# Low halves of the weight tiles made by adding transfers from DRAM instead of by VectorE, in a hybrid encoder layer on one core

## The chip, the core and the metric

The kernel runs on one core of a Trainium2 chip. The metric is the device time of one execution in microseconds. The core's engines that matter here are TensorE (PE: matrix products), VectorE (DVE), ScalarE (ACT), GpSimd (POOL) and SyncE (SP), which issues most transfers; ScalarE and GpSimd can issue transfers too.

## The reference

One layer of a streaming encoder, in single precision, for 1024 prompt tokens and 32 tokens of a running stream (1056 in all), width 1024:

```python
h = _rmsnorm(x, norm_mix_g)
proj = jnp.einsum('bld,de->ble', h, w_in)          # 1024 -> 5136 columns
# A: y_a = a_b * causal_conv3(a_c * a_v)
# B: conv4 and silu on xbc, a Mamba-2 scan in chunks, gated RMSNorm with z
# C: gated unit, causal 31-tap convolution, LayerNorm, silu
x = x + jnp.einsum('ble,ed->bld', jnp.concatenate([y_a, y_b, y_c], axis=-1), w_out)
h2 = _rmsnorm(x, norm_ffn_g)
up, gate = jnp.split(jnp.einsum('bld,df->blf', h2, w_up), 2, axis=-1)
g_conv, new_f = _causal_dwconv(gate, st_f, conv_ffn_w)
x = x + jnp.einsum('blf,fd->bld', jax.nn.silu(g_conv) * up, w_down)   # 2816 -> 1024
```

A final RMSNorm follows, and the last inputs of each convolution and the scan's state are outputs too.

## The kernel before

Features lie on the 128 partitions, tokens along the free axis in three chunks of 256, 384 and 416. The matrix work is cut into *units*: 128 columns of a weight matrix by 1024 rows (a block of 512 KB; for `w_down` 128 rows by 1024 columns). There are 122 such units and one small one for the step widths, numbered in the order of the program: 0 to 19 the inputs of groups A and C, 20 the step widths, 21 to 32 the scan's x, B and C, 33 to 40 z, 41 to 48 the first half of the output projection (`o1`), 49 to 56 its second half (`o2`), then the FFN: two pairs of gate and up, the two `w_down` units of the pair before, two gates and ups again, and so on, with four down units at the end (119 to 122).

Every product of single precision is made of three products of a rounded format: with weights w = hi + lo and tokens x = xH + xL, `three` (L243 to L250) adds hi·xH (L245), hi·xL (L249) and lo·xH (L250) for each of the eight 128x128 blocks k of a unit. A unit is so 72 products. For a down unit the same three stand at L1236, L1237 and L1238, and its eight blocks are the eight output features m, taken in turn for all three chunks; two down units go together, block by block.

The halves are made by `convert` (L180 to L206) from a raw block that `load` (L165 to L178) has brought by a transfer on SyncE's queue: ScalarE rounds the raw block to `hi` (L205), then VectorE makes `lo` as raw minus `hi` (L200). Unit 0 alone is done by VectorE entirely. `weights` (L208 to L216) converts the next unit at the start of this unit's product; in front of a pair of down units two are converted at the start of the pair's second up product. `first_products` (L580 on) takes the first four units chunk by chunk while the next tokens are still prepared, so units 1 to 3 are converted close to each other. The units of `o1` take their blocks in the order 4 to 7, then 0 to 3 (L1130).

Raw blocks, `hi`, `lo` and token rows all live in a common pool of `SLOTS` = 44 tiles of about 4 KB per partition; a new tile waits until the users of the slot's earlier tile are done.

Around it: background work (convolutions, the scan) is put in small steps between the chunks of products, by a table of shares (`PUMP`). The scan fetches a tile `E` by a transfer and masks it on GpSimd (L819), and makes `xe` on GpSimd (L856); GpSimd also copies the state of a convolution into the buffers' heads (L475, L477: `gb` in the FFN) and the last inputs out (L482, L483). A scheduler sets each engine's order from the program's order; each engine then works through its own list in order, waiting for semaphores.

## Time and profile before

| | |
|---|---|
| time, median of 2 runs | 1555.62 us (1555.62 to 1555.63) |
| the profiled execution, first to last instruction | 1557.1 us, 23101 instructions |
| mean granted TensorE clock | 0.994 |
| TensorE busy | 1532.8 us (98%) |
| VectorE busy | 970.5 us (62%) |
| ScalarE busy | 467.5 us (30%) |
| GpSimd busy | 88.3 us (6%) |
| SyncE's and other hardware queues | 117.95 MB, 25.8% of 16 DMA engines |

Busy times count the instructions of an engine; issuing a transfer is not counted. A timeline row reads: start in us, duration in us, engine, line, operation, out<-in, shape, count, and in brackets how long the engine sat idle before it and what it waited for. "ACT hi L205" as a releaser is ScalarE's instruction that wrote `hi` on line 205. Rows with "SPq" or "ACTq" are issues of transfers: the time is that of the issuing, not of the transfer.

### The profile page before, as it was taken

How to read it: one execution, taken by the hardware profiler on the slowest of the kernel's cores; microseconds unless marked ns; L12 is line 12 of the kernel's file. 1: busy time of each engine (PE TensorE's matmuls, PEld its weight loads, DVE VectorE, ACT ScalarE, POOL GpSimd, SP SyncE). 2: the span in 40 equal slices, each digit the busy share in tenths (PEclk: the TensorE clock that was granted, in tenths of full speed). 3: DMA queues.
4: the chain of work that ended last, by engine and by line, in shares of the span. 5: the costliest groups of instructions: out<-in, count | busy, mean ns of one | idle time of the engine just before them, and what ended most of it. 6: DMA issues, size and time to landing. Idle time of an engine off the chain costs nothing.

```text
span 1557.1 us, 23101 instructions
## 1 busy us (share of the span) xinstructions
PE 1532.8 (98%) x9677; PEld 1502.3 (96%) x9677; DVE 970.5 (62%) x1397; ACT 467.5 (30%) x754; POOL 88.3 (6%) x213
## 2 busy tenths in 40 slices
PE   7999999999999899999999999999999999999998
PEld 7999999999999889999999999999999999999997
DVE  7467979599577479686654644545453544546455
ACT  6412112443656365153321120302111121202122
POOL 0000100011122021000000000000000000000000
PEclk9999999999999999999999999999999999999999
DMA  5603011311344577551211111111111111111102
GB/s 175 205 28 109 16 55 45 79 41 41 87 114 100 138 221 187 163 188 55 70 40 41 55 41 41 55 41 55 41 41 41 55 41 55 41 41 55 41 15 112
DMA packets 156758, 119.42 MB, mean 77 GB/s; under 512 B 9045, under 2 KB 145135, under 8 KB 156655
## 3 DMA queue, kind: packets, MB, share of 16 engines
q1 hardware_dynamic: 156639, 117.95, 25.8%
q8 instruction: 76, 1.25, 0.3%
q14 instruction: 27, 0.22, 0.0%
q10 hardware_dynamic: 16, 0.00, 0.0%
HBM read 97.08 MB, written 20.86 MB: 76 GB/s over the span
## 4 chain that ended last, share of the span: by engine, by line
PE 62%; DMA 1%; DVE 0%; ACT 0%; issue 0%; POOL 0%; SPq 0%; DVEq 0%; ACTq 0%; POOLq 0%
PE g L250 12%; PE g L245 12%; PE g L249 12%; PE g L1238 4%; PE g L1236 4%; PE g L1237 4%; PE xT L250 3%; PE xT L249 3%; PE xT L245 3%; PE xT L1236 1%; PE xT L1238 1%; PE xT L1237 1%; DMA zr<-zd 0%; DMA E<-acd 0%; PE yd L893 0%; PE st L883 0%
## 5 line engine op out<-in xcount | busy, mean ns | idle before, releaser
L245 PE MATMUL g<-hH,hi 128*128 128x416 f32 (+2 forms) x952 | 309.7, 325 | 0.0
L250 PE MATMUL g<-hH,lo 128*128 128x416 f32 (+2 forms) x952 | 307.3, 323 | 0.0
L249 PE MATMUL g<-hL,hi 128*128 128x416 f32 (+2 forms) x952 | 307.3, 323 | 0.0
L249 PE MATMUL g<-fL,hi 128*128 128x384 f32 (+2 forms) x792 | 255.9, 323 | 0.0
L250 PE MATMUL g<-fH,lo 128*128 128x384 f32 (+2 forms) x792 | 255.6, 323 | 0.0
L245 PE MATMUL g<-fH,hi 128*128 128x384 f32 (+2 forms) x792 | 255.6, 323 | 0.0
L245 PEld LDWEIGHTS g<-hH,hi 128*128 128x128 f32 x952 | 179.8, 189 | 1.8 <-issue 1.2
L249 PEld LDWEIGHTS g<-hL,hi 128*128 128x128 f32 x952 | 179.8, 189 | 0.4
L250 PEld LDWEIGHTS g<-hH,lo 128*128 128x128 f32 x952 | 179.6, 189 | 0.5 <-DVE lo L200 0.2
L290 DVE SCALAR_TENSOR_TENSOR cacc<-cb,par,cacc 128x1086 f32<-128x1086 f32 (+1 forms) x120 | 159.2, 1327 | 7.3 <-ACT cacc L287 5.7
L200 DVE TENSOR_TENSOR lo<-raw,hi 128x1024 fp32r<-128x1024 f32 x122 | 149.2, 1223 | 21.0 <-ACT hi L205 20.9
L249 PEld LDWEIGHTS g<-fL,hi 128*128 128x128 f32 x792 | 149.4, 189 | 0.4 <-issue 0.2
L250 PEld LDWEIGHTS g<-fH,lo 128*128 128x128 f32 x792 | 149.4, 189 | 0.5 <-issue 0.2
L245 PEld LDWEIGHTS g<-fH,hi 128*128 128x128 f32 x792 | 149.4, 189 | 0.3
L285 ACT ACTIVATE ca<-gb,par 128x1058 f32<-128x1058 f32 x22 | 26.0, 1182 | 407.8 <-DVE gb L1198 407.8
L1240 DVE TENSOR_TENSOR res<-res,g 128x416 f32<-128x416 f32 (+2 forms) x186 | 96.2, 522 | 60.7 <-PE g L1238 54.4
L1236 PE MATMUL g<-mH,hi 128*128 128x384 f32 (+2 forms) x396 | 129.0, 326 | 0.0
L1238 PE MATMUL g<-mH,lo 128*128 128x384 f32 (+2 forms) x396 | 128.5, 324 | 0.0
L1237 PE MATMUL g<-mL,hi 128*128 128x384 f32 (+2 forms) x396 | 128.0, 323 | 0.0
L205 ACT ACTIVATE hi<-raw 128x1024 fp32r<-128x1024 f32 x121 | 124.3, 1046 | 11.4 <-DMA raw<-in_w_in_dram 6.7
L1198 DVE TENSOR_TENSOR gb<-g,rf 128x384 f32<-128x384 f32 (+2 forms) x77 | 29.7, 410 | 142.4 <-PE g L250 142.4
L250 PE MATMUL xT<-fH,lo 128*128 128x256 f32 (+2 forms) x264 | 85.1, 323 | 0.0
(331 smaller groups left out, 2627.5 us busy)
## 6 DMA issues: line engine op xcount, KB each, us to landing
raw<-in_w_up_dram SPq DMA_DIRECT2D x44, 512.0 KB
raw<-in_w_in_dram SPq DMA_DIRECT2D x40, 512.0 KB
raw<-in_w_down_dram SPq DMA_DIRECT2D x22, 512.0 KB
E<-acd SPq DMA_DIRECT2D x16, 512.0 KB
xTd<-xn SPq DMA_DIRECT2D x8, 528.0 KB
zr<-zd SPq DMA_DIRECT2D x8, 528.0 KB
xm<-xTd SPq DMA_DIRECT2D x8, 528.0 KB
res<-r1d SPq DMA_DIRECT2D x8, 528.0 KB
```

The lines of the kernel that those rows point to most:

```text
L200: v.tensor_tensor(out=lo, in0=r, in1=hi.bitcast(F32), op=ALU.subtract)
L205: act.activation(hi, r, AF.Copy)
L245: pe.matmul(o, hi[:, k, :], x, start=first, stop=False)
L249: pe.matmul(o, hi[:, k, :], y, start=False, stop=False)
L250: pe.matmul(o, lo[:, k, :], x, start=False, stop=last)
L285: act.activation(out[:, u:u + n], buf[:, b:b + n], AF.Copy, scale=w_of(0))
L290: v.scalar_tensor_tensor(out=out[:, u:u + n], in0=buf[:, b + j:b + j + n], scalar=w_of(j), in1=out[:, u:u + n], op0=ALU.mult, op1=ALU.add)
L1198: v.tensor_tensor(out=buf[:, b:b + n], in0=ps[:, o:o + n], in1=rf[:, c0 + o:c0 + o + n], op=ALU.mult)
L1236: pe.matmul(o, hi[:, m, :], a[:, c0:c0 + w], start=(f == some[0]), stop=False)
L1237: pe.matmul(o, hi[:, m, :], b[:, c0:c0 + w], start=False, stop=False)
L1238: pe.matmul(o, lo[:, m, :], a[:, c0:c0 + w], start=False, stop=(f == some[-1]))
L1240: v.tensor_tensor(out=rc, in0=rc, in1=o, op=ALU.add)
```

## The change

The function `convert` no longer calls VectorE for `lo` (but for unit 0). ScalarE writes minus `hi` into `lo`, and four transfers on GpSimd's queue each read two of the unit's eight blocks (128 KB) from the weights in DRAM again and add them onto that: lo = -hi + w. So `lo` becomes ready in four pieces, and the product of a block waits for its own piece. The raw block has one reader less. The pool has 43 slots instead of 44, and `dynamic_dma_scratch_size` is 2048 instead of 1024. The lines after the function stand five lines further down than before. (The diff also removes all comments; those lines are left out here.)

```diff
-SLOTS = 44
+SLOTS = 43
...
             act.activation(hi, r, AF.Copy)
-            low()
+            act.activation(lo, hi.bitcast(F32), AF.Copy, scale=-1.0)
+            q3 = lo.rearrange("p (k m) -> p k m", m=P)
+            srcs = units[n][2]
+            for j in range(0, 8, 2):
+                s = srcs[j // 4][:, j % 4:j % 4 + 2, :] if len(srcs) == 2 else srcs[0][:, j:j + 2, :]
+                pool.dma_start(out=q3[:, j:j + 2, :], in_=s, accum_op=ALU.add)
...
-    nc = _bacc.Bacc("TRN2", target_bir_lowering=False, num_devices=1, dynamic_dma_scratch_size=1024)
+    nc = _bacc.Bacc("TRN2", target_bir_lowering=False, num_devices=1, dynamic_dma_scratch_size=2048)
```

The order of the instructions in three places. First ScalarE where two down units (65 and 66) are converted, at the start of the up product of unit 64; `ca` and `pf` are tiles of the FFN's gate and product, the L1203 row is the SiLU. Before:

```order
L205 ACTIVATE hi64_7897<-raw64_7714 128x1024 [waits DMAHW6_49,PE_49]
L285 ACTIVATE ca_7895<-gb_7892,par_77 128x1058 [waits DVE_49,Activation_49,Pool_49]
L205 ACTIVATE hi65_7992<-raw65_7807 128x1024 [waits DMAHW7_49,PE_49]
L205 ACTIVATE hi66_7996<-raw66_7901 128x1024 [waits DMAHW0_49,Activation_49]
L1203 ACTIVATE ca_7895<-ca_7895 128x1058 [waits DVE_49]
L1218 ACTIVATE mH3_8081<-pf_7896 128x1056 [waits DVE_49,Activation_49]
```

And of the change:

```order
L205 ACTIVATE hi64_8145<-raw64_7958 128x1024 [waits DMAHW6_49]
L206 ACTIVATE lo64_8146<-hi64_8145 128x1024 [waits Activation_49]
L290 ACTIVATE ca_8143<-gb_8140,par_77 128x1058 [waits DVE_49,PE_49,Pool_49]
L205 ACTIVATE hi65_8244<-raw65_8055 128x1024 [waits DMAHW7_49]
L206 ACTIVATE lo65_8245<-hi65_8244 128x1024 [waits Activation_49]
L205 ACTIVATE hi66_8252<-raw66_8153 128x1024 [waits DMAHW0_49,PE_49]
L1208 ACTIVATE ca_8143<-ca_8143 128x1058 [waits DVE_49]
L206 ACTIVATE lo66_8253<-hi66_8252 128x1024 [waits DMASW1_49,DMASW2_49,DMASW0_49,DMASW3_49,PE_49,Activation_49]
```

Each rounding is now followed by a negation, and the SiLU of the gate stands between the rounding and the negation of the second down unit. Next GpSimd at the same place. Before, it only fills and empties the heads of the convolution's buffers:

```order
L482 COPY fpack_7330<-gb_7705 128x2 [waits DVE_49]
L483 COPY fpack_7330<-gb_7705 128x2 [waits DVE_49]
L475 MEMSET gb_7892 128x2 [waits PE_49,Activation_49]
L477 COPY gb_7892<-par_77 128x2
L482 COPY fpack_7330<-gb_7892 128x2 [waits DVE_49]
L483 COPY fpack_7330<-gb_7892 128x2 [waits DVE_49]
```

And of the change:

```order
L487 COPY fpack_7554<-gb_8140 128x2 [waits DVE_49]
L488 COPY fpack_7554<-gb_8140 128x2 [waits DVE_49]
L211 DMA lo65_8245<-in_w_down_dram 128x256 [waits DMASW4_49,Activation_49,Pool_49]
L211 DMA lo65_8245<-in_w_down_dram 128x256 [waits DMASW5_49]
L211 DMA lo65_8245<-in_w_down_dram 128x256 [waits DMASW6_49]
L211 DMA lo65_8245<-in_w_down_dram 128x256 [waits DMASW7_49]
L211 DMA lo66_8253<-in_w_down_dram 128x256 [waits DMASW0_49,Activation_49]
L211 DMA lo66_8253<-in_w_down_dram 128x256 [waits DMASW1_49]
L211 DMA lo66_8253<-in_w_down_dram 128x256 [waits DMASW2_49]
L211 DMA lo66_8253<-in_w_down_dram 128x256 [waits DMASW3_49]
L480 MEMSET gb_8547 128x2 [waits DMAHW0_49]
L482 COPY gb_8547<-par_77 128x2
```

Eight transfers stand in a row there, the second unit's behind the first one's, and the next buffer's head behind all eight. Each transfer waits for the one that stood eight transfers earlier (DMASW0 to DMASW7 are their semaphores). Last GpSimd in the scan, where the first units of `o1` (41 and 42) are converted. Before, it has only the scan's own tiles there:

```order
L856 TENSOR_TENSOR xe_5075<-xd_5071,dend_2363 128x512 [waits DVE_49]
L856 TENSOR_TENSOR xe_5148<-xd_5144,dend_2363 128x512 [waits DVE_49]
L819 AFFINE_SELECT E_5112<-E_5112 128x1024 [waits DMAHW0_49]
L819 AFFINE_SELECT E_5264<-E_5264 128x1024 [waits DMAHW7_49,Activation_49]
L856 TENSOR_TENSOR xe_5313<-xd_5309,dend_2363 128x512 [waits DVE_49]
```

And of the change:

```order
L861 TENSOR_TENSOR xe_5235<-xd_5231,dend_2443 128x512 [waits DVE_49]
L861 TENSOR_TENSOR xe_5308<-xd_5304,dend_2443 128x512 [waits DVE_49]
L211 DMA lo41_5119<-in_w_out_dram 128x2x128 [waits DMASW4_49,Activation_49]
L211 DMA lo41_5119<-in_w_out_dram 128x2x128 [waits DMASW5_49]
L211 DMA lo41_5119<-in_w_out_dram 128x2x128 [waits DMASW6_49]
L211 DMA lo41_5119<-in_w_out_dram 128x2x128 [waits DMASW7_49]
L861 TENSOR_TENSOR xe_5477<-xd_5473,dend_2443 128x512 [waits DVE_49]
L824 AFFINE_SELECT E_5272<-E_5272 128x1024 [waits DMAHW0_49]
L211 DMA lo42_5326<-in_w_out_dram 128x2x128 [waits DMAHW6_49,DMASW0_49,Activation_49]
L211 DMA lo42_5326<-in_w_out_dram 128x2x128 [waits DMASW1_49]
L211 DMA lo42_5326<-in_w_out_dram 128x2x128 [waits DMASW2_49]
L211 DMA lo42_5326<-in_w_out_dram 128x2x128 [waits DMASW3_49]
```

The transfers of a unit stand between the scan's tiles, behind an `xe` that waits for VectorE and an `E` that waits for its own transfer.

## Rows read from the trace of the kernel before

**Rows 1.** The page, busy us of each engine (share of the span), instructions.

```profile
PE 1532.8 (98%) x9677; PEld 1502.3 (96%) x9677; DVE 970.5 (62%) x1397; ACT 467.5 (30%) x754; POOL 88.3 (6%) x213
```

**Rows 2.** The page, groups: count | busy, mean ns of one | idle before, releaser.

```profile
L250 PEld LDWEIGHTS g<-hH,lo 128*128 128x128 f32 x952 | 179.6, 189 | 0.5 <-DVE lo L200 0.2
...
L200 DVE TENSOR_TENSOR lo<-raw,hi 128x1024 fp32r<-128x1024 f32 x122 | 149.2, 1223 | 21.0 <-ACT hi L205 20.9
...
L205 ACT ACTIVATE hi<-raw 128x1024 fp32r<-128x1024 f32 x121 | 124.3, 1046 | 11.4 <-DMA raw<-in_w_in_dram 6.7
```

**Rows 3.** Windows: stretch and us, busy by engine (instructions), clock, DMA share, GB/s.

```profile
5.00:20.00 15.00, 10.24 (x61) 9.97 (x62) 11.91 (x24) 8.57 (x19) 0.00 (x0) 1.00 1.06 370
...
960.00:1000.00 40.00, 40.00 (x256) 39.92 (x255) 15.40 (x23) 8.32 (x8) 0.79 (x6) 1.00 0.14 40
```

**Rows 4.** Timelines of SyncE, ScalarE and GpSimd: issues, their first readers, one mask.

```profile
0.80 1.82 SPq L310 DMA_DIRECT2D x<-in_x_prompt_dram  x4
...
3.51 0.63 ACT L430 ACTIVATE hx<-x 128x512 f32<-128x512 f32 x1 [0.60 <-DMA x<-in_x_prompt_dram]
...
37.31 1.02 SPq L177 DMA_DIRECT2D raw<-in_w_in_dram  x2
...
41.12 1.06 ACT L205 ACTIVATE hi<-raw 128x1024 fp32r<-128x1024 f32 x1 [5.83 <-DMA raw<-in_w_in_dram]
...
557.43 1.80 POOL L819 TENSOR_SCALAR_AFFINE_SELECT E<-E 128x1024 f32<-128x1024 f32 x1 [6.26 <-DMA E<-acd]
```

**Rows 5.** GpSimd's lines (mean; min/median/max of L477), one copy, VectorE beside it.

```profile
L856 POOL TENSOR_TENSOR xe<-xd,dend 128x512 f32<-128x512 f32 (+1 forms) x18 | 20.2, 1123 | 63.2 <-DVE xd L850 63.2
...
L477 POOL COPY gb<-par x22: 185/191/995, 770.6 to 1460.4; 128x2 f32<-128x2 f32 x22
...
862.69 0.99 POOL L477 COPY gb<-par 128x2 f32<-128x2 f32 x1
...
862.42 1.22 DVE L200 TENSOR_TENSOR lo<-raw,hi 128x1024 fp32r<-128x1024 f32 x1
```

**Rows 6.** Timelines, a single FFN unit: its rounding, its first product with `lo`.

```profile
847.01 1.04 ACT L205 ACTIVATE hi<-raw 128x1024 fp32r<-128x1024 f32 x1
...
856.86 0.28 PE L250 MATMUL g<-fH,lo 128*128 128x256 f32 x1
```

**Rows 7.** Timelines, a down pair: roundings, SiLU, first product with the second `lo`.

```profile
858.68 1.99 ACT L205 ACTIVATE hi<-raw 128x1024 fp32r<-128x1024 f32 x2
862.53 1.09 ACT L1203 ACTIVATE ca<-ca 128x1058 f32<-128x1058 f32 x1 [1.86 <-DVE ca L290]
...
868.77 0.28 PE L1238 MATMUL g<-mH,lo 128*128 128x256 f32 x1
```

**Rows 8.** Timelines of the start: roundings of units 1 and 3, first `lo`, unit 3's end.

```profile
14.08 1.05 ACT L205 ACTIVATE hi<-raw 128x1024 fp32r<-128x1024 f32 x1
...
22.73 1.11 ACT L205 ACTIVATE hi<-raw 128x1024 fp32r<-128x1024 f32 x1
...
17.98 0.28 PE L250 MATMUL g<-hH,lo 128*128 128x256 f32 x1
...
28.08 0.43 DVE L561 TENSOR_TENSOR ua<-g,vt 128x256 f32<-128x256 f32 x1 [0.54 <-PE g L250]
```

**Rows 9.** Timelines, first and last of units 41 to 44: rounding, first product with `lo`.

```profile
546.73 1.05 ACT L205 ACTIVATE hi<-raw 128x1024 fp32r<-128x1024 f32 x1
...
551.45 0.70 PE L250 MATMUL g<-oH,lo 128*128 128x256 f32 x2
...
594.23 1.05 ACT L205 ACTIVATE hi<-raw 128x1024 fp32r<-128x1024 f32 x1
...
599.91 0.28 PE L250 MATMUL g<-oH,lo 128*128 128x256 f32 x1
```

**Rows 10.** Timelines, the last four down units: last two roundings, first product with last `lo`.

```profile
1496.16 1.99 ACT L205 ACTIVATE hi<-raw 128x1024 fp32r<-128x1024 f32 x2
...
1504.42 0.35 PE L1238 MATMUL g<-mH,lo 128*128 128x416 f32 x1
```

## Prediction

> **What bounds the kernel now.** I read four things in this order. First the busy times of the page: TensorE works in 1532.8 of 1557.1 us [rows 1]. All its waiting together is 24 us, 1.6% of the span, so a change that only takes waiting away cannot reach 2% (31 us; about what a measurement of this kernel can tell from no change). VectorE, which the change relieves, is 62% busy and ScalarE, which gets new work, 30% [rows 1]. Second, who waits for VectorE's `lo`: TensorE's weight loads waited for it 0.2 us in the whole run, although the 122 subtractions take 149.2 us of VectorE [rows 2]. Third, a stretch of the FFN by windows: between 960 and 1000 us TensorE is busy 40.00 of 40, VectorE 15.40, ScalarE 8.32 and the DMA engines 0.14 [rows 3]. So VectorE's subtraction is hidden already, and what the change can do is to make `lo` late. Fourth, the timelines of the units whose `lo` is needed soonest after `hi` was made: the start, the first o1 units, the pairs of down units, the last four.
>
> **What is removed.** 121 of the 122 subtractions on VectorE (1223 ns each, 148 us in all). Nothing on TensorE's path waits for them, so I take 0 for it. At best the shorter queue on VectorE also pulls in the few us that TensorE waits in the scan; that is a rival below.
>
> **What is added on ScalarE.** 121 activations of 128x1024, the same shape and engine as the rounding (1046 ns [rows 2]): 127 us more, 30% to 38%. Each stands right behind its `hi` on a mostly idle engine, so it delays `lo` by 1.05 us and hardly anything else.
>
> **What is added on GpSimd and the DMA queues.** 4 x 121 = 484 adding transfers of 128 KB. No row of before shows a GpSimd transfer or an adding one, so two durations have to be bounded.
>
> G, the time for which GpSimd is held by one issue. From below: SyncE's issues of 256 KB, four in 1.82 us, 0.45 us each [rows 4]. From above: the longest GpSimd whole-tile operation near here, 1.80 us [rows 4]. A transfer of GpSimd's here has 128 x 2 pieces of 512 bytes; if GpSimd has to go through them, that is nearest to one of its own tile operations, 1123 ns for 128x512 [rows 5]. SyncE's issues are those of another engine, so I take G = 1.1 us.
>
> L, from the end of an issue until TensorE may use the block. The first 256 KB half of x: its issue ends at 0.80 + 0.45 = 1.25, its reader starts at 3.51: 2.25 us. A 512 KB weight load: issue ends at 37.31 + 0.51 = 37.82, reader at 41.12: 3.3 us [rows 4]. The straight line through both gives 1.7 us for 128 KB, the lower end. An adding transfer has to read the 128 KB it adds to as well, so it moves like 256 KB, 2.25 us; with a little for the add I take L = 2.5 us, and 3.3 us is the upper end.
>
> The first block of a unit is then ready 1.05 (`hi`) + 1.05 (negation) + 1.1 + 2.5 = 5.7 us after `hi` starts, each further block 1.1 us later. Before, `lo` was whole after 1.05 + 1.22 = 2.3 us. Now the places.
>
> *Single units.* In the FFN a unit's `hi` starts at 847.01 and its first `lo` product at 856.86 [rows 6]: 9.8 us for 5.7, and the other blocks are needed 0.9 us apart at first (six products of 0.16 us: 256 in 40.00 us [rows 3]) and arrive 1.1 us apart, the last at 9.0. Covered: **0**. The cover is the conversion one unit ahead.
>
> *Pairs of down units.* Nine times, two down units are converted at the start of one up product: `hi` and `hi` in 858.68 to 860.67, the second one's `lo` first used at 868.77 [rows 7]. GpSimd's order now has eight transfers in a row there. The first can be issued at 858.68 + 2.1 = 860.8, the fifth (first block of the second unit) ends its issue 5 G later and lands after L: 860.8 + 5.5 + 2.5 = 868.8. That is level with the use, no margin. (ScalarE's order has the SiLU between `hi` and negation of the second unit; it ended at 863.62 [rows 7], the negation then at 864.7, before GpSimd is through with the first unit at 865.2, so it adds nothing unless VectorE, for which it waits, is later than before.) I take 0.3 us for each pair, **+3**. Here the sum hangs on G: each 0.1 us of it costs 0.5 us in nine places. The blocks behind are needed 5.6 us apart (36 products) and are in time.
>
> *Start.* Twelve issues, for units 1 to 3. `hi` of unit 1 runs from 14.08 to 15.13, its negation to 16.2; its `lo` was used from 17.98 [rows 8]. From 16.2 GpSimd is the limit: 16.2 + 12 x 1.1 + 2.5 + 0.9 (six products behind the last block) = 32.8 for the end of unit 3 in the first chunk; it was 28.1, where VectorE's wait for that product ends [rows 8]. `hi` of unit 3 ends at 23.84, its negation at 24.9, before GpSimd comes free for it (25.0), so it isn't the limit. That is +4.7. The DMA engines are full of the first loads between 5 and 20 us (share 1.06 [rows 3]), so I take **+6**. Ends: with G 0.45 and L 1.7, unit 3 is bound by its negation, 24.9 + 1.8 + 1.7 + 0.9 = 29.3, +1; with 1.8 and 3.3, +14.
>
> *First o1 units.* Units 41 to 44 are taken in the order of blocks 4 to 7, then 0 to 3, so the third transfer is needed first: 1.05 + 3.3 + 2.5 = 6.9 us after `hi` ended. The room was 3.7 us for the first of the four (547.78 to 551.45) and 4.6 for the last (595.28 to 599.91) [rows 9]; over the four I add up some 11 us. Their transfers also stand behind the scan's `xe` and `E` on GpSimd, as the order shows. Against this, a late unit lets the next conversion start no later, and the scan's own products fill part: **+7**, ends 0 and 20.
>
> *Last four down units.* `hi` of the last two from 1496.16, the second one's `lo` used at 1504.42 [rows 10]: 1496.16 + 2.1 + 5.5 + 2.5 = 1506.3, **+2**.
>
> *DMA engines.* Between 960 and 1000 us 40 GB/s, 1.6 MB, about three units of 512 KB, take 0.14 x 40 = 5.6 us, 1.9 us per unit [rows 3]. Read twice, the added bytes take 3.7 us. Together 5.6 of the 11.3 us that a unit's 72 products take: covered, 0.
>
> *One slot less* (43): `raw` comes free after `hi` and not after `lo`, which gives it back: 0.
>
> Sum 3 + 6 + 7 + 2 = +18 on the profiled 1557.1: 1575. That execution stands 1.5 us above the median of the runs shown, 1555.62, so I forecast **1573.5 us**, +1.1%. An us more of G costs 45 (pairs) + 12 (start) + 12 (o1) + 5 (end) = 74 us; an us more of L 9 + 1 + 4 + 1 = 15. The forecast passes +2% (13 us further) at G = 1.28 or at L = 3.4.
>
> **The rivals.**
> A, hidden: with G near 0.45 the pairs have 3 us to spare, the start costs 1 and o1 nothing: 1556 to 1558; if VectorE's relief then gives back the scan's few us, 1550. For it: the FFN's room [rows 6] and the DMA engines' idleness. Against: the 0.45 us is another engine's. The Trainium skill, page "DMA: Bandwidth & Descriptors", section "Anatomy of one DMA — SWDGE (gpsimd) path", gives a GpSimd transfer about 2.0 us plus its bytes over 436 GB/s, that is 2.3 us for 128 KB by my estimate; no transfer of that kind is in this trace, and with it in place of G + L = 3.6 the sum comes to about nought.
>
> B, slower by GpSimd's issue time: at G = 1.8 the pairs cost 9 x 3.5 = 32 more, start and o1 8 each, the end 4: 18 + 52 = +70, 1626. It decides from 1.28 us. For it: each transfer has 256 pieces, and GpSimd's longest operations reach 1.8; against: its mean ones are near 1.1.
>
> C, slower by VectorE: GpSimd's tiny copy into `gb` takes 0.19 us in most of 22 cases and up to 0.99; the one at 862.69 lies under a subtraction of VectorE that runs from 862.42 to 863.64 [rows 5]. So some two-input operations of VectorE hold GpSimd off. In a pair's stretch VectorE still runs three two-input operations of that size after the change (two taps of the convolution, L290, and a product, L1205). If issuing is held likewise, up to 3 x 1.22 = 3.7 us x 9 = 33 more: 1607; it decides from 1.4 us per pair (13 / 9). Against: the copy reads and writes tiles, and no row shows that an issue does. The Trainium skill, page "SBUF — State Buffer", section "SBUF: two separate sides", has such a lock, and says that a transfer issued by GpSimd waits for its list while VectorE runs an operation in a mode that takes both ports; the two-input ones hold only GpSimd operations that read. The 0.99 us agree with the lock; that it reaches an issue no run here shows yet.
>
> D, slower by the adding itself: if an add costs the engines over five times a plain transfer, 1.9 + 6 x 1.9 = 13.3 us a unit pass the 11.3, and 121 units pay 2.0 each: 1555.6 + 242 = about 1800. Nothing in the rows speaks for more than twice.
>
> **How the numbers follow.** Forecast (+6 to +30) 0.46; A 0.14; B, from 1.28 us on, 0.20; C 0.13; D 0.07. Predicted is the likeliest, 1573.5. The range takes in A's common part and B's end: 1553 to 1630, with D and the best of A and some of B and C together outside it. The likeliest one's own range is 1561 to 1586. Faster by over 2% would need more than all waiting: 0.01. Within 2%: forecast and A, 0.59. Slower: B, C, D, 0.40.
>
> **What would show it.** G: the distance of GpSimd's transfers in a pair (1.1, against 0.45 or 1.8). L: from an issue's end to the first product with that block, waits of TensorE put down to DMA `lo`. Start: the end of unit 3's first chunk at 32 to 34 instead of 28.1. FFN: windows with TensorE at 40.00 of 40 except a fraction of a us before each second down unit; gaps of 3 us there speak for B or C, C if they come with VectorE's two-input operations. VectorE's busy time should fall by 148 us, ScalarE's rise by 127, and neither should show in the time. Wrong at once: time lost in the single units, which I call covered.

## The result, and the profile after

The changed kernel takes 1629.47 us (median of 2 runs, 1627.61 to 1631.33) against 1555.62: 1.0473 times the time, interval 1.0443 to 1.0504. The profiled execution spans 1629.6 us. The forecast of 1573.5 was 56 us short: the loss, 74 us where 18 were forecast, has the forecast's sign but four times its size, and the largest part of it lies where the forecast had put nothing.

The page after, engines' busy times and the new queue of GpSimd (packets, MB, share of 16 engines):

```profile
PE 1552.6 (95%) x9677; PEld 1517.1 (93%) x9677; DVE 848.8 (52%) x1276; ACT 593.9 (36%) x877; POOL 644.8 (40%) x697
...
q0 software_dynamic: 120384, 63.47, 31.4%
```

Against [rows 1], VectorE lost 122 us of busy time, where 148 were forecast, and ScalarE gained 126, as forecast. GpSimd went from 6% to 40%; in this count its 484 issues are included, other than those of SyncE and ScalarE. TensorE has the same 9677 products and is busy 19.8 us longer: some ran at the lower clock. The other 53 us of the 72.5 between the two profiled executions are idle time. Who TensorE waits for (total, times, longest, us):

```profile
PE g L255 <- DMA lo<-in_w_out_dram: 16.7, 4, 7.0
PE g L255 <- DMA lo<-in_w_in_dram: 15.0, 5, 6.4
PE g L1087 <- DVE diag L1085: 6.4, 1, 6.4
...
PE g L250 <- ACT zs L1099: 5.7, 2, 4.5
PE g L1243 <- DMA lo<-in_w_down_dram: 4.5, 8, 1.5
PE g L493 <- POOL bpack L487: 4.0, 1, 4.0
```

The first two are pieces of `lo`, nearly all for o1 (14.6 us) and for the start (12.5). Three others were not waits of before at all: a VectorE, a ScalarE and a GpSimd result of the work beside the products. Windows show where (columns as in [rows 3]):

```profile
0.00:40.00 40.00, 18.48 (x96) 16.83 (x97) 13.14 (x34) 18.56 (x40) 14.47 (x23) 0.83 0.75 195
...
560.00:600.00 40.00, 30.08 (x179) 25.40 (x177) 16.93 (x27) 15.34 (x32) 8.69 (x7) 0.83 0.61 151
...
960.00:1000.00 40.00, 40.00 (x248) 39.91 (x247) 14.37 (x22) 13.44 (x13) 14.68 (x21) 1.00 0.38 69
```

The FFN is as full as in [rows 3], 40.00 of 40. The start and the scan's stretch have holes, and in both the granted clock is 0.83.

To place the loss, I took from each trace the end of the last product of some units and subtracted that of before (us behind; last product of the unit named):

| kernel | time, us | unit 19 (start, A, C) | 32 (xbc) | 40 (z) | 48 (o1) | 64 (o2, first FFN) | 118 (nine down pairs) | 122 |
|---|---|---|---|---|---|---|---|---|
| the change | 1629.5 | 15.8 | 20.3 | 44.8 | 61.9 | 64.1 | 70.8 | 72.5 |
| start_vector | 1616.4 | -0.8 | 3.8 | 28.5 | 45.4 | 48.2 | 55.8 | 59.5 |
| scan_vector | 1590.2 | 16.5 | 16.5 | 21.8 | 17.5 | 20.6 | 27.7 | 29.9 |
| scan_half | 1603.2 | 16.2 | 16.2 | 26.9 | 33.9 | 39.6 | 45.4 | 47.0 |
| lists_4096 | 1620.3 | 14.6 | 18.2 | 35.1 | 52.6 | 53.0 | 61.4 | 64.0 |
| scan_two_ahead | 1619.5 | 17.4 | 17.4 | 37.2 | 43.9 | 45.5 | 53.5 | 55.7 |
| fixed_unread_adds | 1579.5 | 3.9 | 3.9 | 16.6 | 20.0 | 22.0 | 22.0 | 21.9 |
| fixed_unread_copies | 1569.1 | 0.6 | 0.6 | 10.2 | 9.2 | 11.7 | 11.7 | 11.7 |
| unread_adds | 1630.1 | 17.3 | 17.3 | 51.9 | 63.6 | 68.9 | 68.9 | 68.9 |
| unread_copies | 1588.0 | 11.1 | 11.1 | 25.6 | 27.8 | 28.4 | 28.4 | 28.4 |
| copies_by_sync | 1592.4 | 13.2 | 13.2 | 29.5 | 32.3 | 34.0 | 34.0 | 33.9 |
| gpsimd_busy | 1571.3 | 5.4 | 5.4 | 15.1 | 14.4 | 14.5 | 14.5 | 14.5 |
| spare_tile_only | 1566.2 | -0.2 | -0.2 | 5.4 | 7.1 | 7.0 | 7.0 | 7.0 |
| negate_then_vector | 1566.9 | -0.3 | -0.3 | 7.3 | 8.3 | 8.2 | 8.2 | 8.2 |
| gate_up_only | 1558.6 | -1.0 | -1.0 | 0.9 | 2.2 | 2.2 | 2.2 | 2.1 |
| scan_off_gpsimd | 1631.8 | 16.3 | 19.6 | 37.5 | 55.2 | 58.4 | 66.0 | 68.5 |
| skip_vector_late | 1626.3 | 11.3 | 16.3 | 37.2 | 54.1 | 59.2 | 65.1 | 66.9 |

So of the change's 72.5: the start 15.8, units 21 to 48 46.1, o2 2.2, the nine down pairs 6.7, the end 1.7. Units 4 to 19 lose nothing. The other rows are the experiments below. Most medians have two or three timed runs behind them and each row of the table one profiled execution; the runs of the change itself differ by 4 us, those of scan_off_gpsimd and scan_two_ahead by 8 and 9, so differences of 3 us say little.

What TensorE does in units 21 to 40 and in 41 to 48, first before, then in the change (columns as in [rows 3]; the windows run from the end of one unit to that of another):

```profile
254.57:536.82 282.25, 281.82 (x1841) 271.75 (x1840) 206.63 (x267) 139.14 (x265) 36.32 (x64) 1.00 0.33 83
536.82:679.37 142.55, 135.69 (x910) 124.26 (x908) 108.92 (x161) 69.11 (x122) 19.15 (x17) 0.95 0.65 192
```

```profile
270.37:581.66 311.29, 290.86 (x1841) 279.61 (x1840) 186.22 (x245) 161.99 (x288) 130.15 (x142) 0.96 0.59 110
581.66:741.23 159.57, 139.91 (x910) 127.84 (x908) 102.68 (x151) 77.39 (x130) 64.86 (x53) 0.91 0.82 198
```

Units 21 to 40 take 29.0 us more: 20.0 us are idle time of TensorE and 9.0 the same products at a lower clock. Of the idle time only 2.4 us end with a piece of `lo`. Units 41 to 48 take 17.0 us more, 12.8 idle and 4.2 by the clock, and here 14.6 us end with a piece.

### The profile page after: what moved, and what is told of

The parts are those of the page before. It is cut to its first block, busy times and chain, and to the rows that moved or that the text cites. A ratio compares the mean times of both kernels' runs of the same rounds, so it can differ in the third digit from the quotient of the medians.

```text
span 1629.6 us, 24048 instructions
## 1 busy us (share of the span) xinstructions
PE 1552.6 (95%) x9677; PEld 1517.1 (93%) x9677; DVE 848.8 (52%) x1276; ACT 593.9 (36%) x877; POOL 644.8 (40%) x697
## 3 DMA queue, kind: packets, MB, share of 16 engines
q0 software_dynamic: 120384, 63.47, 31.4%
q8 instruction: 76, 1.25, 0.3%
## 4 chain that ended last, share of the span: by engine, by line
PE 79%; DMA 8%; issue 4%; POOL 3%; ACT 3%; DVE 2%; SPq 0%; ACTq 0%; POOLq 0%; DVEq 0%
PE g L250 18%; PE g L255 18%; PE g L254 18%; PE g L1243 4%; PE g L1241 4%; PE g L1242 4%; POOL lo L211 3%; DMA lo<-in_w_down_dram 3%; PE xT L254 2%; PE xT L255 2%; PE xT L250 2%; DMA E<-acd 2%; PE xT L1241 1%; PE xT L1243 1%; PE xT L1242 1%
## 5 line engine op out<-in xcount | busy, mean ns | idle before, releaser
L255 PE MATMUL g<-hH,lo 128*128 128x416 f32 (+2 forms) x952 | 312.0, 328 | 15.1 <-DMA lo<-in_w_in_dram 15.0
L250 PE MATMUL g<-hH,hi 128*128 128x416 f32 (+2 forms) x952 | 313.7, 330 | 5.7 <-ACT zs L1099 5.7
L254 PE MATMUL g<-hL,hi 128*128 128x416 f32 (+2 forms) x952 | 311.2, 327 | 0.0
L211 POOL DMA_DIRECT2D lo<-in_w_up_dram x176 | 215.7, 1527 | 172.0 <-ACT lo L206 153.2
L211 POOL DMA_DIRECT2D lo<-in_w_in_dram x156 | 193.4, 1523 | 170.2 <-ACT lo L206 108.0
L255 PEld LDWEIGHTS g<-hH,lo 128*128 128x128 f32 x952 | 183.5, 193 | 16.9 <-DMA lo<-in_w_in_dram 16.4
L250 PEld LDWEIGHTS g<-hH,hi 128*128 128x128 f32 x952 | 183.5, 193 | 7.9 <-ACT zs L1099 6.2
L254 PEld LDWEIGHTS g<-hL,hi 128*128 128x128 f32 x952 | 183.6, 193 | 0.3
L206 ACT ACTIVATE lo<-hi 128x1024 fp32r<-128x1024 f32 x121 | 128.1, 1058 | 3.2
```

Of the source, the lines that this page charges most:

```text
L206: act.activation(lo, hi.bitcast(F32), AF.Copy, scale=-1.0)
L211: pool.dma_start(out=q3[:, j:j + 2, :], in_=s, accum_op=ALU.add)
L250: pe.matmul(o, hi[:, k, :], x, start=first, stop=False)
L254: pe.matmul(o, hi[:, k, :], y, start=False, stop=False)
L255: pe.matmul(o, lo[:, k, :], x, start=False, stop=last)
```

## The experiments

The theories. *Late pieces*: TensorE waits because its own `lo` comes late (the forecast's view). *Held list*: GpSimd, held by its transfers, lets the scan's mask, `xe` and state copies wait. *Crowded engines*: the added traffic itself slows every transfer in the stretches where the DMA engines were already busy. Late pieces turned out to have a share of their own, and the other two together another; how these two divide it stays open.

### Where: VectorE's subtraction back in one stretch

```diff
+            if n < FIRST:            # start_vector;  21 <= n <= 48: scan_vector;
+                low()                # n < 57 or units[n][0] == "down": gate_up_only
+                return
             act.activation(lo, hi.bitcast(F32), AF.Copy, scale=-1.0)
```

> The change, but units 1 to 3 get their lo from VectorE as before. In the trace of the change unit 3 (and so the whole program) is 15.8 us behind by the end of the first units: TensorE waits 5.7, 6.4 and 0.4 us for pieces of lo, and its granted clock is 0.83 there. If the start's loss is its own (nothing later depends on it), this gives 1629 - 16 = about 1613 us. If the rest of the program merely runs into the same waits later (the loss is shared by a resource that stays behind), it stays near 1625.

1616.35 us, near the 1613 named, and the start's loss is gone (-0.8). It is the start's own.

> The change, but units 21 to 48 (the scan's inputs, z and the first half of the output projection, the stretch in which the scan runs) get their lo from VectorE as before. There the program falls 46 us further behind (lag 15.8 us before it, 62 after unit 48). If the loss belongs to these units, 1629 - 46 = about 1583 us. If VectorE's relief is what keeps the scan from being worse, some of it comes back and the time is above 1590.

1590.18: by the trace the loss of units 21 to 48 falls from 46.1 to 1.0. The time lies on the line drawn for VectorE's relief, so it says nothing of that. These two stretches hold 62 of the 72.5 us.

> The change for the 44 gate and up units of the FFN alone; all others (start, projections, output projection, down units) get their lo from VectorE. The forecast called these units covered: a block is needed 9.8 us after its rounding starts and ready after 5.7. So the time is that of before, 1556 to 1559 us. If the single units of the FFN lose too, or if VectorE's relief gives something back there, it is 3 us or more away from that.

1558.61 us, ratio 1.0015 (1.0003 to 1.0026). With transfers for 44 units of the FFN nothing is lost there and nothing won (the 2 us in the table arise in units 21 to 48, where this run has of the change only its 43 slots); between 960 and 1000 us the engines stand at 40.00 of 40 as before:

```profile
960.00:1000.00 40.00, 40.00 (x255) 39.92 (x254) 12.11 (x21) 8.54 (x9) 10.66 (x14) 1.00 0.38 79
```

### How many transfers are under way

GpSimd at the start of the change (timeline), and the first two of TensorE's waits there:

```profile
15.88 3.79 POOL L211 DMA_DIRECT2D lo<-in_w_in_dram  x3 [14.12 <-ACT lo L206]
22.99 1.22 POOL L211 DMA_DIRECT2D lo<-in_w_in_dram  x1 [3.32 <-issue]
24.42 2.43 POOL L211 DMA_DIRECT2D lo<-in_w_in_dram  x2 [0.21 <-issue]
33.72 2.44 POOL L211 DMA_DIRECT2D lo<-in_w_in_dram  x2 [6.87 <-issue]
...
22.77 0.58 PE L255 MATMUL g<-hH,lo 128*128 128x256 f32 x1 [5.71 <-DMA lo<-in_w_in_dram]
...
33.50 0.58 PE L255 MATMUL g<-hH,lo 128*128 128x256 f32 x1 [6.45 <-DMA lo<-in_w_in_dram]
```

Three are issued, then GpSimd stands still until the first has landed (TensorE starts with it at 22.77, GpSimd goes on at 22.99). In the whole trace no more than three transfers of 512-byte pieces are under way, and no more than seven of `w_down`'s 1 KB pieces.

```diff
-    nc = _bacc.Bacc("TRN2", ..., dynamic_dma_scratch_size=2048)
+    nc = _bacc.Bacc("TRN2", ..., dynamic_dma_scratch_size=1024)    # lists_1024; 4096: lists_4096
```

> The change with dynamic_dma_scratch_size 1024. Theory 'held queue': one transfer of 512-byte pieces at a time (three of 1 KB): a unit takes 4 x (1.2 + 2.3 + 0.3) = 15 us, more than its 11.3 us of products, so all units but the down units are bound by it: 100 x 3.9 us more, about 2000 us. If the limit of three is not set by this size (a fixed depth), no change: 1625 to 1632.

2055.83 us, near the 2000 expected. One at a time, with 2.6 us of standing still between them, for 512-byte pieces; three at a time for `w_down`:

```profile
1406.91 2.70 POOL L211 DMA_DIRECT2D lo<-in_w_down_dram  x3 [2.96 <-issue]
...
1420.15 1.22 POOL L211 DMA_DIRECT2D lo<-in_w_up_dram  x1 [2.25 <-ACT lo L206]
1423.97 1.22 POOL L211 DMA_DIRECT2D lo<-in_w_up_dram  x1 [2.59 <-issue]
```

> The change with dynamic_dma_scratch_size 4096 instead of 2048. In the change never more than three transfers of 512-byte pieces (seven of 1 KB pieces) are under way at once, and the next one is issued 0.3 us after one has landed. Theory 'held queue': that limit comes from this size, GpSimd is held by it, and so are the scan's mask and xe behind: with twice the size six or seven are under way, no transfer waits for a landing within a unit, and the scan's stretch gains 10 to 25 us: 1605 to 1620. Theory 'crowded engines': the DMA engines are what is slow, the pieces land at the same times: 1625 to 1632.

1620.27 (1617.69 to 1622.86). All eight at the start go out in one row, yet that stretch keeps 14.6 of its 15.8 us:

```profile
15.22 10.12 POOL L211 DMA_DIRECT2D lo<-in_w_in_dram  x8 [13.48 <-ACT lo L206]
```

So the size sets the limit, and the limit itself costs about 9 us of the 73, in the scan.

### Pieces that nobody reads, first attempt: a spare tile of the pool

VectorE makes `lo` again; the change's negation and transfers go to a pool tile that nobody reads:

```diff
             act.activation(hi, r, AF.Copy)
+            low()
+            dup = slot(1024, F32R, name=f"dup{n}")
-            act.activation(lo, hi.bitcast(F32), AF.Copy, scale=-1.0)
-            q3 = lo.rearrange("p (k m) -> p k m", m=P)
+            act.activation(dup, hi.bitcast(F32), AF.Copy, scale=-1.0)
+            q3 = dup.rearrange("p (k m) -> p k m", m=P)
```

> VectorE makes every lo as before; ScalarE's negation and the 484 adding transfers of the change are kept with the same places and waits, but go to a spare tile of the pool that nobody reads. So the traffic, GpSimd's list and ScalarE's work are those of the change, and no product waits for a piece. Theory 'late pieces': nearly all of the 73 us is TensorE waiting for its pieces: 1556 to 1565 us. Theory 'held list': the scan's mask, xe and the state copies on GpSimd stand behind transfers, and loads of E and of the raw blocks share the DMA engines: the 30 us or so of waits for VectorE, ScalarE and GpSimd stay: 1580 to 1600 us.

1630.06 us, above both ranges and as slow as the change, although no product reads a transferred piece. I took this for the proof of *crowded engines*. The trace shows another reason: `dup` holds a slot of the 43 until its transfers have landed, and the next owner of the slot waits for that. The longest waits for `dup`, other than those of the transfers themselves (us, times):

```profile
  DVE cen L784: 19.3, 2
  DVE lo L200: 16.1, 1
```

In the change nothing of the kind happens: its slot comes free when the products have read it. So this run, and the next four, which have the same tile, tell less than they were made for.

```diff
-                pool.dma_start(out=q3[:, j:j + 2, :], in_=s, accum_op=ALU.add)
+                pool.dma_start(out=q3[:, j:j + 2, :], in_=s)      # unread_copies
+                dma(out=q3[:, j:j + 2, :], in_=s)    # copies_by_sync, without the negation
```

> As the run with unread adding transfers, but each of them is a plain copy of the same bytes (no add). Measures what the adding itself costs a transfer: the forecast took 2.25 us of moving for an add against 1.7 for a plain one, and the DMA engines' share for the added bytes twice that of a plain load. If adding is what fills the engines, the share of GpSimd's queue (31.4% of 16 engines in the change) is about half here, and pieces of a full queue land 0.3 us apart instead of 0.65. If not, both are unchanged. Time: at or below the run with unread adding transfers.

1588.02 us. Who waits for `dup` waits less: 12.4 us `cen`, 11.1 us `lo`, 1.6 us `xn`. GpSimd's queue carries the same bytes in a fifth of the packets and 13.0% of the engines' time, against 31.4% in the change, and one issue is shorter (ns, min/median/max):

```profile
q0 software_dynamic: 23232, 63.47, 13.0%
...
L213 POOL DMA_DIRECT2D dup<-in_w_up_dram x176: 712/722/739, 792.1 to 1506.1; - x176
```

> VectorE makes every lo; the same blocks of weights are read a second time into a spare pool tile that nobody reads, as plain copies issued by SyncE instead of GpSimd (no negation, no add). The same plain bytes as in the run with unread copies by GpSimd (1588 us), without GpSimd. Theory 'crowded engines': the traffic alone costs, 1575 to 1590 us. Theory 'held list': about that of the control, 1556 to 1562.

1592.35 us, just above the range named for *crowded engines* and near the copies by GpSimd, which has nothing more to do here than before. Again slots are waited for (14.8 us `lo`, 12.6 us `xn`), so this doesn't show that GpSimd is innocent.

```diff
+            low()                                     # the change's lines for lo are gone
+            dup = slot(1024, F32R, name=f"dup{n}")
+            act.activation(dup, hi.bitcast(F32), AF.Copy, scale=-1.0)
+            for _ in range(5):                        # gpsimd_busy; without these two
+                pool.memset(dup.bitcast(F32), 0.0)    # lines: spare_tile_only
```

> As the control, with five whole-tile memsets on GpSimd per unit (about 0.95 us each, 4.8 us per unit) in the place of the four transfers (4 x 1.2 us), still with no transfer: GpSimd's list is as full as in the change, and the DMA engines carry what they did before. Theory 'held list': the scan's loss of the unread transfers is GpSimd's occupation, and comes back here: 1580 us or more. Theory 'crowded engines': as the control, within 5 us of it.

1571.33 us.

> Control for the runs with unread transfers: VectorE makes every lo, ScalarE writes the negation into a spare pool tile that nobody reads, and there are no transfers. So only ScalarE's 127 us and the one more tile of the pool per unit are left. If these are harmless, as the forecast said of ScalarE, 1556 to 1562 us; what it has above 1557 must be taken off the unread runs before anything is put down to transfers.

1566.21 us, ratio 1.0064 (1.0041 to 1.0087). GpSimd, occupied for about as long as by the issues (658.5 us busy, 644.8 in the change), so costs 5 us by the medians and 7.5 by the traces, most of it at the start (5.4 in the table): a list that is merely full is not the large loss. It doesn't stand and wait for landings here, as it does in the change. And the control isn't harmless itself. To tell its pool tile from ScalarE's work, one run without the tile:

```diff
             act.activation(lo, hi.bitcast(F32), AF.Copy, scale=-1.0)
+            v.tensor_tensor(out=lo, in0=r, in1=lo.bitcast(F32), op=ALU.add)    # no transfers
```

> ScalarE writes minus hi into lo as in the change, then VectorE adds the raw block onto it in place: the change's work on ScalarE, before's work on VectorE (one longer chain), 43 slots, no transfers and no spare tile. The control with a spare tile took 1566, 10.6 us over before. If ScalarE's extra 127 us are what costs there (in the scan it was busy 33 of 40 us between 560 and 600 us), 1564 to 1568 here; if it is the extra tile of the pool, 1556 to 1559.

1566.93 us: the loss stays without the tile, 8.6 us in units 21 to 48, nearly all of it up to unit 40. Besides ScalarE's 127 us this run has one link more in the chain to `lo`, and 43 slots without the early release of the raw block. The slots alone cost 1.0 us there in scan_vector and 3.2 in gate_up_only, so some 5 to 8 us are left for the negations and the longer chain, against the forecast's "hardly anything else".

### The traffic alone: a fixed spare tile

The same 484 transfers, now to 3 KB per partition outside the pools, without a negation. Each is still kept behind what landed on its part of the tile earlier; it needs no `hi` and so may go out earlier than in the change.

```diff
+        SPARE = const.tile([P, 768], F32R, name="spare")
...
-            act.activation(lo, hi.bitcast(F32), AF.Copy, scale=-1.0)
-            q3 = lo.rearrange("p (k m) -> p k m", m=P)
+            low()
+            q3 = SPARE.rearrange("p (k m) -> p k m", m=P)
...
-                pool.dma_start(out=q3[:, j:j + 2, :], in_=s, accum_op=ALU.add)
+                d = q3[:, j % 6:j % 6 + 2, :]
+                tc.keep_in_program_order(pool.dma_start(out=d, in_=s, accum_op=ALU.add))
+                # fixed_unread_copies: pool.dma_start(out=d.bitcast(F32), in_=s)
```

> VectorE makes every low half as before, and GpSimd issues all 484 adding transfers to one fixed spare tile that nobody reads and that takes no slot of a pool; there is no negation. Late pieces (the loss of the runs with unread transfers was the slot that the unread tile held): 1556 to 1562 us. Crowded engines (the traffic by itself slows the scan's other transfers): 1575 to 1610 us, with 20 to 45 us of it in the scan.

1579.45 us, ratio 1.0148 (1.0119 to 1.0178).

> The same as the run with unread adds to a fixed tile, with plain copies: less than half of the engines' time. Late pieces: 1556 to 1562 us. Crowded engines: 1562 to 1575 us, about 10 us lost in the scan.

1569.06 us, ratio 1.0082 (1.0052 to 1.0111). So of the 64 us that the first attempt lost over its control, most went with the tile of the pool. The traffic with GpSimd's part in it costs 22 us: 3.9 at the start, 16.1 in units 21 to 48, 2 in the o2 units, and in the FFN with its pairs nothing, though all 484 transfers run. Copies cost 12. Windows of before, and of the run with unread adds:

```profile
40.00:120.00 80.00, 80.00 (x486) 78.13 (x485) 42.62 (x51) 22.86 (x34) 1.00 (x6) 1.00 0.34 115
440.00:480.00 40.00, 40.00 (x275) 36.67 (x274) 35.56 (x43) 27.35 (x56) 8.57 (x7) 1.00 0.57 129
560.00:640.00 80.00, 79.20 (x566) 72.64 (x565) 70.72 (x107) 44.08 (x86) 14.17 (x13) 1.00 0.66 186
```

```profile
40.00:120.00 80.00, 80.00 (x480) 78.06 (x479) 40.78 (x52) 21.32 (x32) 32.37 (x39) 1.00 0.71 156
440.00:480.00 40.00, 36.62 (x233) 33.73 (x230) 28.82 (x38) 22.76 (x47) 16.09 (x14) 0.91 0.65 128
560.00:640.00 80.00, 72.96 (x493) 65.90 (x493) 68.55 (x98) 45.19 (x85) 37.29 (x32) 0.95 0.94 219
```

In the scan the engines were fuller already before than in the FFN (0.14), and their share goes from 0.57 to 0.65 and from 0.66 to 0.94. But the share alone isn't what costs: between 40 and 120 us, where no scan runs, it goes from 0.34 to 0.71 and TensorE stays at 80.00 of 80, while 12.7 of the 16.1 us are lost in units 33 to 40. TensorE's longest waits in that run, but for one of the start, are for VectorE's and GpSimd's results in the scan:

```profile
PE g L253 <- DVE r L1135: 5.9, 3, 2.4
PE misc L847 <- DVE E L882: 4.3, 1, 4.3
PE st L891 <- POOL xe L864: 4.3, 3, 2.0
```

Is that the engines or GpSimd's list? Both are in it: in this kernel GpSimd waits for earlier landings, and `xe` behind such a wait. The scan's loads of `E` are hardly later at the median: where the mask waited for the landing alone, it began 7.0 us after the issue before (13 cases, 8.8 the longest), 6.7 in this run (13, 12.5) and 7.1 in the change (11, 11.2). How the 16 us split between them stays open.

### Half the transfers, and the scan's work off GpSimd

```diff
-            for j in range(0, 8, 2):
+            for j in range(0, 8, 4 if 21 <= n <= 48 else 2):    # the other blocks by VectorE
```

> The change, with half of the blocks of units 21 to 48 (the scan's stretch) made by VectorE and half by two adding transfers instead of four. All by transfers loses 46 us there (1629), all by VectorE leaves 1590. If the traffic is what costs, about half of the 39 us between them comes back: 1605 to 1615. If what costs is that a unit waits for its slowest piece at all, little comes back (1620 or more); if only the third and fourth piece are late, nearly all of it (1590 to 1600).

1603.21 us (1600.54 to 1605.88): units 21 to 48 lose 17.7 with half of the transfers, 46.1 with all, 1.0 with none. The loss grows more than in proportion; traffic, GpSimd's hold, ScalarE's negations and the number of pieces that can be late all halve here, so the run doesn't tell them apart.

```diff
-            pool.affine_select(out=e3[0:q], ..., fill=-1e30, ...)
+            v.tensor_tensor(out=e3[0:q], in0=e3[0:q], in1=neg..., op=ALU.add)
-            pool.tensor_tensor(out=xe[0:q]..., 
+            v.tensor_tensor(out=xe[0:q]...,
```

> The change, with the scan's mask of E and its xe moved from GpSimd to VectorE, which the change has relieved (36 operations of 1.1 to 1.3 us). GpSimd's list in the scan then has only transfers and the small state copies. Theory 'held list' (transfers of lo and the scan's tiles wait for each other on GpSimd): the loss of units 33 to 48 (about 36 us) falls by 10 to 25 us: 1605 to 1620. Theory 'crowded engines' (pieces and E land late because of the DMA engines): no gain, 1625 to 1632.

1631.76 us (1627.79 to 1635.73): no gain in time. Its profiled execution, the faster of the two, loses 35.6 us in units 33 to 48 where the change loses 41.6, less than the 10 to 25 us expected. So the mask and `xe` behind the transfers are not the large part, as far as a run can show it that puts the same work on VectorE. Another thing on GpSimd's list does cost: at unit 33 the loss grows by 6.1 us (20.3 to 26.5), and the chain of waits of the change shows why:

```profile
422.26 0.95 ACT hi L205
...
423.59 0.95 ACT lo L206
...
424.94 3.63 POOL lo L211 x3
...
429.52 1.77 POOL bpack L487
...
431.33 0.61 PE g L493 x2
```

The copy into `bpack` for the convolution's state stands behind the issues on GpSimd, and TensorE waits 4.0 us for it.

The two longest waits of units 33 to 40, of 6.4 us (at L1087) and 4.5 us (for `zs`, L1099), have another chain. It goes back from both through the scan's work to loads of `E`:

```profile
521.11 6.49 DMA E<-acd
...
555.07 7.57 DMA E<-acd
```

These landed in about the time that such a load took before, so why the scan reached them late is not shown.

### More lead for the pieces

```diff
         def weights(n, ahead=1):
+            if 20 <= n <= 46:
+                ahead = max(ahead, 2)
             convert(n)
```

> The change as it is, but in units 20 to 46 the conversion (rounding, negation, adding transfers) runs two units ahead of the products and not one; the traffic is the same and holds GpSimd as long. Late pieces: TensorE's waits for pieces of o1 (16.7 us) and the few of xbc mostly go, the stretch of units 21 to 48 loses 46 - 15 to 20 = 26 to 31 us, the time is 1605 to 1618. Crowded engines and held lists alone: no change, 1625 to 1633. Slower than 1635 if the further ahead piece's slots or order stop something else.

1619.51 us (1614.51 to 1623.64), ratio 1.0405 (1.0366 to 1.0444), 10 us less than the change and 1.5 above the time named for late pieces; its profiled execution, of 1612.8 us and the fastest of three, has no wait of TensorE for a piece in the scan's stretch any more (of the change: 17.0 us), only those of the start and of the pairs:

```profile
PE g L257 <- DMA lo<-in_w_in_dram: 12.7, 3, 6.7
PE g L1245 <- DMA lo<-in_w_down_dram: 7.8, 10, 2.0
```

Units 21 to 48 lose 26.5 us by it, instead of 46.1. So late pieces cost something like the 17 us that TensorE waited for them, 10 by the medians. The 20 us between the traces are not all pieces: 9.2 of them come back in units 21 to 40, where only 2.4 us were waited for pieces. The waits for other things stay, 23 us in the change and 28 here, partly on other tiles.

### The small load at the start

The transfers issued at 22.99 to 25.33 us in the change moved nothing until 30, with the DMA engines all but idle (a share of 0.06 between 25 and 30 us). In that time a load of `d_skip` runs in 1024 pieces of 4 bytes.

> The change, with one small load made differently: d_skip is brought as 64 bytes per partition and picked apart by VectorE, not as 1024 pieces of 4 bytes (L473). In the change's trace the adding transfers issued at 22.99, 24.42 and 25.33 us move nothing until 30.0, while some 107 pieces a microsecond of almost no bytes run and the engines' share is 0.05; they land at 33.5 to 34.9. Theory 'stuck behind small pieces': without them these land by 28, and the start's loss falls from 15.8 to about 8 us: about 1622. If the small pieces are not what they wait for, no change at the start, 1626 to 1632.

1640.15 us, slower: VectorE's new picking apart stood ahead of the first products and waited 15 us for its load. But the fourth transfer landed at 27.6 instead of 33.5. So once more, with the picking put later (the diff of both):

```diff
-                dma(out=dskip[64 * half:64 * half + 64, :],
-                    in_=d_skip[0].rearrange("(t h) -> h t", h=2)[half].partition_broadcast(64))
+            dma(out=dsk, in_=d_skip[0].partition_broadcast(P))
+                v.tensor_copy(dskip[64 * half:64 * half + 64, :],   # skip_vector_late: behind unit 20
+                              dsk[64 * half:64 * half + 64, :].rearrange("p (t h) -> p h t", h=2)[:, half, :])
```

> The change, with d_skip brought as 64 bytes per partition and picked apart by VectorE only after the first projections, so that VectorE's list at the start is the change's own (the run before had the picking in front of the first products, which then waited 13 us for it, though the fourth transfer landed at 27.6 us instead of 33.5). If the 1024 pieces of 4 bytes are what holds the transfers at the start, unit 3 is 8 to 10 us behind before instead of 15.8, and the time is 1619 to 1623. If not, 1626 to 1632.

1626.26 us, at the edge of "no" by time; by its trace the start loses 11.3 us instead of 15.8, and GpSimd goes on at 28.82 where it had stood until 33.72:

```profile
24.38 3.68 POOL L211 DMA_DIRECT2D lo<-in_w_in_dram  x3 [4.38 <-issue]
28.82 2.49 POOL L211 DMA_DIRECT2D lo<-in_w_in_dram  x2 [0.75 <-issue]
```

So by this trace the 4-byte pieces cost the start some 4.5 us, less than expected. The first piece is not helped: it lands at 24 us, behind the loads of x.

## Why the prediction was wrong, step by step

**The sum.** By the table the forecast's 3 (pairs), 6 (start), 7 (o1) and 2 (end) measured 6.7, 15.8, 17.1 and 1.7. To these come 29.0 in units 21 to 40 and 2.2 in o2, for which it had 0.

**Right.** VectorE's 148 us were worth nothing: no stretch of the table gains. G: 1.1 was taken; an issue of a 512-byte-piece transfer measures 1.22 us at the median, one of `w_down`'s 0.89. The single units of the FFN are covered, and so are units 4 to 19. The last four down units cost 1.7. Minima, medians and maxima of an issue in ns, and under them from issue to landing in us, over all 484:

```profile
L211 POOL DMA_DIRECT2D lo<-in_w_up_dram x176: 1203/1223/2257, 822.0 to 1550.0; - x176
...
DMA to landing us min/median/max: 2.8/4.5/11.0
```

**L was a constant.** The forecast took 2.5 us from an issue's end, in the end 3.3 at most. In quiet the lower value is right: 3.5 us from an issue's start in the FFN, that is 2.3 from its end. But the maximum is 11.0 from an issue's start (9.25 from its end), and all that took over 5 us from an issue's end lie before 721 us: at the start, in units 4 to 19 (up to 7.0, without harm there) and in the scan. I had read the DMA engines at 1.06 between 5 and 20 us [rows 3] and put 1.3 us on the start for it; the wait of GpSimd's mask for `E` in [rows 4] hinted at the same for the scan, and I used that row only for a duration. One case, unit 43 (timelines of the change: ScalarE, GpSimd, SyncE, TensorE):

```profile
629.41 1.04 ACT L205 ACTIVATE hi<-raw 128x1024 fp32r<-128x1024 f32 x1
...
632.07 1.05 ACT L206 ACTIVATE lo<-hi 128x1024 fp32r<-128x1024 f32 x1
...
633.53 3.69 POOL L211 DMA_DIRECT2D lo<-in_w_out_dram  x3 [4.68 <-ACT lo L206]
...
634.36 0.39 SPq L823 DMA_DIRECT2D E<-acd  x1
...
637.20 1.45 SPq L1121 DMA_DIRECT2D xm<-xTd  x1
...
646.11 0.55 PE L255 MATMUL g<-oH,lo 128*128 128x256 f32 x1 [7.04 <-DMA lo<-in_w_out_dram]
...
643.00:648.00 5.00, 1.89 (x9) 1.92 (x10) 0.14 (x1) 3.87 (x10) 3.21 (x4) 0.50 0.68 161
```

The negation comes 1.6 us after the rounding's end, with the scan's exponential between. The third transfer, the one that is needed first, ends its issue at 637.2; `E` and `xm` go out on the same engines in that time, and it lands just before 646.11, nearly 9 us later. TensorE has waited 7.04 us, and the granted clock is 0.50 (1.2 GHz) afterwards. The clock's part I had left out: 19.8 us of longer products in all. The term for o1 was 7 (ends 0 to 20) and measured 17.1, with 14.6 us of waits for pieces.

**"Single units: covered, 0" was read from one FFN unit and applied to units 21 to 40.** They lost 29 us (15.8 to 44.8), the largest wrong step, and what the forecast itself had named as "wrong at once". In the FFN it is right, and in units 4 to 19. In units 21 to 40 the pieces themselves are nearly in time: TensorE waits 2.4 us for them. But the same transfers and negations meet a scan whose loads, masks and copies use the same engines and the same lists, and the forecast had no term for what that does to the scan: TensorE waits 17.6 us more than before for other things, the scan's results above all (20.0 less 2.4), and 9.0 us come from the lower clock. What the scan loses it by is only partly known. Single runs give 12.7 us in units 33 to 40 for traffic with GpSimd's hold (the fixed tile with adds), 5 to 8 us for ScalarE's negations with the longer chain, and 4.0 us for one copy behind the issues. These overlap, so they are no sum, and the rest stays open.

**"DMA engines: 5.6 of 11.3 us, covered" was read from one stretch.** Adding takes 2.4 times a plain copy's engine time (31.4% to 13.0%), near the factor 2 that was taken. But the engines were unevenly busy: 0.14 in the window that it went by [rows 3], 0.57 between 440 and 480 us and 0.66 between 560 and 640 us of before, windows that the forecast did not use. There the same transfers, with GpSimd's hold, cost something although nobody reads them.

**The start** (forecast 6, measured 15.8): the first piece landed at 22.7 and not at 19.8, behind the loads of x; then the limit of three, which no row of before shows, and the 4-byte pieces, whose load stands in the trace of before too, without a GpSimd transfer beside it; then the lower clock. Here the pieces are the loss: TensorE waits 12.5 us for three of them, and the same traffic without a reader loses 3.9.

**The pairs** (3, measured 6.7, 0.75 each): the forecast's chain was right to 0.5 us, but by luck. `w_down`'s pieces go out faster than taken (eight in 7.16 us) and land later (0.65 us apart, the fifth 3.5 us after its issue's end); in the pair at 925.58 us the fifth landed 8.0 us after the first was issued, and 5 G + L were 8.0 too.

**The rivals.** A didn't come: G was not 0.45. B's time (1626) came out, but not by B: G is 1.22, and the decision at 1.28 was not passed. That the result lies just inside the forecast's range, whose upper end was B's, is luck. C would have cost 3.7 us per pair, where 0.75 were measured. The trace of the change speaks against it too: 66 issues of 512-byte pieces that lay under VectorE's long two-input operations for 95% of their time or more took 1.21 us at the median and 1.25 at most, 237 with none beside them 1.22 and 1.26 (without the time in which GpSimd's instruction before still ran). D's sum did not come: the FFN's gate and up units pay nothing for the adding, and where adding costs more than copying without a reader (22 to 12 us) it is the start and the scan.

The Trainium skill, page "DMA: Bandwidth & Descriptors", section "Anatomy of one DMA — SWDGE (gpsimd) path", would by its figures have 2.3 us for such a transfer, an estimate. Measured were 3.5 us for an add in quiet, and 2.3 at the least and 2.8 at the median for the plain copies of unread_copies. So it agrees with the fastest copies; for the add the measurement decides.

## What to carry to other kernels

A margin read in one stage holds for that stage: before a step is called covered everywhere, read the transfers' engines by windows, and who else stands in the lists of the engines that get the work. An operation saved on an engine that nobody waits for is worth nothing, while a chain of three engines and a queue in its place can need more lead; the lead is then one of the first things to vary (here it gave back 10 of 74 us). A copy of the traffic that nobody reads tells traffic from lateness only if its target isn't waited for either: a tile of a full pool is.

## What the runs showed of the hardware

How many GpSimd transfers are under way is set by `dynamic_dma_scratch_size`: with 1024 one of 256 pieces or three of 128, with 2048 three or seven, with 4096 up to seven or eight (eight semaphores take turns). At the limit, the next one is issued 0.2 to 0.3 us after the first has landed.

An adding transfer stays in packets of its pieces' size, 512 bytes or 1 KB (120384 packets in all), where copies of the same blocks have packets of 4 KB (23232 in all), and GpSimd issues it in 1.22 us against 0.72 for 512-byte pieces. VectorE's two-input operations beside it did not lengthen an issue.

While SyncE's load of 1024 4-byte pieces ran, GpSimd's transfers moved nothing for about 5 us, with the engines' share at 0.06; without that load the fourth transfer landed 3.6 or 4.2 us after its issue and not 10.5. Why they stood still is not settled.
